# Seven block products for the latents' feed-forward up product, and the feed-forward split into two phases

## The chip, the core and the metric

One core of a Trainium2 chip runs the whole program. The metric is the device time of one execution in microseconds (us). PE is TensorE (matmuls; PEld its weight loads), DVE is VectorE, ACT is ScalarE, POOL is GpSimd, SP is the queue that issues the DMAs.

## What is computed

A two-layer backbone over 1,024 latent tokens and 256 context tokens, model width 1,024. Layer 0 mixes tokens with an mLSTM and a Hyena group, layer 1 with a gated DeltaNet and a latent-attention group. After each mixer an output projection and a gated residual give `x`; the part at issue, a convolutional feed-forward, follows:

```python
h = modulate(x, shift, scale)              # RMS norm, then scale and shift
z = dwconv(h @ w_up, conv_w, conv_b)       # 1024 -> 2 x 2816, a 3-tap convolution over tokens
y = silu(z[..., :D_FF]) * z[..., D_FF:]    # gate half and up half, D_FF = 2816
x = x + gate_mod * (y @ w_down)            # 2816 -> 1024
```

Layer 0 computes this for latents and context, layer 1 for the latents alone. All matrices are fp32. The kernel gets fp32 accuracy out of fp32r matmuls by splitting every operand into a rounded high part and a remainder: `hi*hi + hi*lo + lo*hi`, three matmuls for each pair of tiles (`mm3`, lines 229 to 231).

## The kernel before

Features lie on partitions in KT = 8 tiles of 128, tokens along the free dimension. The Tile framework puts each engine's instructions in an order of its own when the program is built: an instruction may go ahead of others that stand before it in the source, when its inputs and its buffer are free by the framework's reckoning. On the chip each engine then runs its list in that fixed order.

`emit_out` (output projection) goes over token chunks of 512, 512 and, in layer 0, 256 context tokens. While one chunk is projected, the RMS norm of the chunk before (`norm_stats`, `norm_apply`) runs in steps between the projections, and writes `h` as a high and a low tile (`hh`, `hl`). The residual `x` of all tokens (`xr`) stays in SBUF through the feed-forward.

`emit_ffn` is one loop over NF = 22 tiles `f` of the 2,816 hidden features. For each f it loads two weight tiles of 128x1024 (gate: tile f; up: tile 22+f), splits each (`load_w`: high part on ACT at line 37, low part on DVE at line 38), and makes the gate and the up product over all tokens in a PSUM tile of three banks (`big`): 8 k-tiles x 3 matmuls for each chunk. `conv3` applies the three taps with one ACT and two DVE instructions straight from PSUM, ACT applies Silu, DVE multiplies gate and up and splits the result into `yh`, `yl`. After every second f the down product of these two f is added to `xr`: for each of 8 output tiles and each chunk 6 matmuls in a PSUM bank (`sm`) and one DVE instruction (line 272). So `y` never leaves SBUF, and each down weight tile (`fdh`, `fdl`) is loaded and split once. The last f writes its up product bank by bank; then the last down blocks are made chunk by chunk, and the next norm (layer 0) or the store of the output (layer 1) is woven into them.

Buffers: raw weights, high and low parts two each (`dw`, tags `wraw`, `wh`, `wl`); PSUM two one-bank tiles (`sm`) and two three-bank tiles (`big`).

Of the kernel before, what the change touches and what calls it, by code (L numbers as in the profile page):

```python
# [8 lines left out]
F32 = mybir.dt.float32  # L9
F32R = mybir.dt.float32r  # L10
# [8 lines left out]
KT = 8  # L19
# [83 lines left out]
def norm_pads(g, h):  # L103
    for t in h:
        for c in (LAT, TP - 1):
            g.nc.gpsimd.memset(t.bitcast(F32)[:, :, c:c + 1], 0.0)


def norm_stats(g, x, chunk, pool, big, res, nm=""):
# [6 lines left out]
    for k in range(KT):  # L116
        q = sq[:, n * (1 + k % nq):n * (2 + k % nq)] if k else acc
        nc.scalar.activation(out=q, in_=x[:, k, c0:c0 + n], func=ACTF.Square)
# [24 lines left out]
def norm_apply(g, layer, which, x, h, chunk, pool, big, res, bufs=1):  # L143
# [82 lines left out]
def mm3(nc, ps, pairs):  # L226
# [7 lines left out]
def dense(g, ps, w, h, chunks, base=0):  # L234
    whi, wlo = w
    hhi, hlo = h
    for c0, n in chunks:
        mm3(g.nc, ps[:, c0 - base:c0 - base + n],
            [(whi[:, 128 * k:128 * k + 128], wlo[:, 128 * k:128 * k + 128], hhi[:, k, c0:c0 + n], hlo[:, k, c0:c0 + n])
             for k in range(KT)])  # L240


def conv3(g, ps, out, cw, cb, n):
    nc = g.nc
    stt = nc.vector.scalar_tensor_tensor
    nc.scalar.activation(out=out[:, :n], in_=ps[:, :n], func=ACTF.Identity, scale=cw[:, 1:2], bias=cb)
    stt(out=out[:, 1:n], in0=ps[:, 0:n - 1], scalar=cw[:, 0:1], in1=out[:, 1:n], op0=ALU.mult, op1=ALU.add)
    stt(out=out[:, 0:n - 1], in0=ps[:, 1:n], scalar=cw[:, 2:3], in1=out[:, 0:n - 1], op0=ALU.mult, op1=ALU.add)  # L248
# [2067 lines left out]
```

## Time and profile before

| | us |
|---|---|
| median of three runs | 3866.21 |
| lowest and highest run | 3851.93, 3870.67 |
| span of the profiled execution (first to last instruction) | 3852.7 |

Of the profiled execution only its span is given, no separate time; the span is 13.5 us below the median of the runs. The feed-forward of layer 0 with its output projection runs from about 1050 to 2120 us of the span, that of layer 1 from about 3009 us to the end. A matmul's duration in the records is longer than the distance from one start to the next, since matmuls are pipelined; the distance is what counts.

### The profile page before, as it was taken

The page shows a single profiled execution, that of the slowest core. Times are in us where ns is not written, and L with a number is a line of the kernel's source. Part 1 is how long each engine was busy: PE and PEld are TensorE (multiplying, and loading weights), DVE is VectorE, ACT ScalarE, POOL GpSimd, SP SyncE. Part 2 cuts the span into 40 slices and gives each one's busy share as a digit, 9 for nine tenths or more (in the row PEclk, how much of TensorE's full clock was granted, in tenths as well). Part 3 has the DMA queues.
Part 4 walks back from the last instruction along what each step waited for, and adds up shares of the span by engine and source line. Part 5 has one row for each costly group of instructions (what it writes and reads, how often), then busy time and mean ns, then how long its engine had stood idle before and what let it go on. Part 6 is the DMA issues. An engine that isn't in the chain of part 4 may idle for free.

```text
span 3852.7 us, 51861 instructions
## 1 busy us (share of the span) xinstructions
PE 3677.6 (95%) x20874; PEld 2982.9 (77%) x20874; DVE 2198.8 (57%) x4198; ACT 1195.1 (31%) x2221; POOL 65.3 (2%) x111
## 2 busy tenths in 40 slices
PE   6999999989999999999998999989999899999999
PEld 3778878866777888888887877767788678888887
DVE  6213566777775445444458584864566565555545
ACT  3323234511142122112224453543445332222121
POOL 0000000000000000000000000000000000000000
PEclk9999999999999999999999999996899899999999
DMA  5443556789731111011111252462355511111111
GB/s 188 129 141 123 161 178 216 215 272 307 254 121 44 39 39 39 33 33 39 44 39 66 75 153 79 143 228 101 114 178 185 181 61 50 50 44 55 39 55 60
DMA packets 303507, 440.20 MB, mean 114 GB/s; under 512 B 19546, under 2 KB 199010, under 8 KB 298276
## 3 DMA queue, kind: packets, MB, share of 16 engines
q1 hardware_dynamic: 293988, 419.07, 33.4%
q0 software_dynamic: 9280, 17.83, 1.6%
q8 instruction: 164, 2.69, 0.3%
q14 instruction: 75, 0.61, 0.0%
HBM read 334.60 MB, written 102.24 MB: 113 GB/s over the span
## 4 chain that ended last, share of the span: by engine, by line
PE 68%; DVE 5%; DMA 3%; ACT 3%; issue 2%; POOL 0%; SPq 0%; ACTq 0%; DVEq 0%; POOLq 0%
PE big L231 10%; PE big L230 10%; PE big L229 10%; PE sm L229 7%; PE sm L230 7%; PE sm L231 7%; PE maS L2005 3%; PE hyp L923 2%; PE hys L1091 1%; PE maT L1125 1%; PE hya L81 1%; DMA mw<-in_mod_w 1%; PE sd L1125 1%; PE maO L229 0%; PE pb L1620 0%
## 5 line engine op out<-in xcount | busy, mean ns | idle before, releaser
L229 PE MATMUL big<-hh,wh 128*128 128x512 f32 (+1 forms) x1728 | 639.1, 371 | 10.4 <-DVE fcg L248 9.9
L231 PE MATMUL big<-hh,wl 128*128 128x512 f32 (+1 forms) x1728 | 640.3, 371 | 0.4 <-DVE wl L38 0.4
L230 PE MATMUL big<-hl,wh 128*128 128x512 f32 (+1 forms) x1728 | 639.8, 371 | 0.1
L38 DVE TENSOR_TENSOR wl<-wraw,wh 128x1024 fp32r<-128x1024 f32 (+1 forms) x168 | 199.5, 1187 | 554.0 <-ACT wh L37 550.9
L229 PE MATMUL sm<-hh,wh 128*128 128x512 f32 (+1 forms) x1192 | 445.8, 376 | 15.7 <-ACT hh L157 5.2
L230 PE MATMUL sm<-hl,wh 128*128 128x512 f32 (+1 forms) x1192 | 441.0, 371 | 3.9 <-DVE hl L158 3.6
L231 PE MATMUL sm<-hh,wl 128*128 128x512 f32 (+1 forms) x1192 | 440.1, 370 | 0.2 <-DVE wl L38 0.2
L272 DVE SCALAR_TENSOR_TENSOR xr<-sm,modT,xr 128x512 f32<-128x512 f32 (+1 forms) x400 | 276.1, 697 | 243.4 <-PE sm L231 243.4
L229 PEld LDWEIGHTS big<-hh,wh 128*128 128x128 f32 x1728 | 325.8, 189 | 68.5 <-issue 5.5
L230 PEld LDWEIGHTS big<-hl,wh 128*128 128x128 f32 x1728 | 326.3, 189 | 59.1 <-DVE hl L158 1.3
L231 PEld LDWEIGHTS big<-hh,wl 128*128 128x128 f32 x1728 | 325.7, 189 | 56.9 <-DVE wl L38 0.7
L37 ACT ACTIVATE wh<-wraw 128x1024 fp32r<-128x1024 f32 (+1 forms) x168 | 172.7, 1028 | 598.0 <-PE big L230 441.7
L229 PE MATMUL sm<-yh,fdh 128*128 128x512 f32 (+1 forms) x800 | 298.1, 377 | 0.0
L230 PE MATMUL sm<-yl,fdh 128*128 128x512 f32 (+1 forms) x800 | 297.0, 373 | 0.0
L231 PE MATMUL sm<-yh,fdl 128*128 128x512 f32 (+1 forms) x800 | 292.5, 372 | 0.0
L229 PEld LDWEIGHTS sm<-hh,wh 128*128 128x128 f32 x1192 | 227.0, 191 | 68.5 <-issue 11.7
L230 PEld LDWEIGHTS sm<-hl,wh 128*128 128x128 f32 x1192 | 227.5, 191 | 46.0 <-DVE hl L158 7.7
L231 PEld LDWEIGHTS sm<-hh,wl 128*128 128x128 f32 x1192 | 227.1, 191 | 36.6 <-issue 0.9
L37 ACT ACTIVATE fdh<-wraw 128x1024 fp32r<-128x1024 f32 x44 | 46.6, 1059 | 555.6 <-PE sm L230 520.9
L229 PEld LDWEIGHTS sm<-yh,fdh 128*128 128x128 f32 x800 | 149.5, 188 | 44.2 <-DVE xr L272 13.8
L230 PEld LDWEIGHTS sm<-yl,fdh 128*128 128x128 f32 x800 | 150.4, 188 | 28.8 <-DVE yl L38 2.7
L231 PEld LDWEIGHTS sm<-yh,fdl 128*128 128x128 f32 x800 | 148.5, 188 | 25.9
(559 smaller groups left out, 6051.4 us busy)
## 6 DMA issues: line engine op xcount, KB each, us to landing
wraw<-in_ffn_up SPq DMA_DIRECT2D x88, 512.0 KB, 3.3
mw<-in_mod_w SPq DMA_DIRECT2D x32, 1024.0 KB, 7.7
wraw<-in_ffn_down SPq DMA_DIRECT2D x44, 512.0 KB, 3.3
dfw<-in_dft POOLq DMA_DIRECT2D x32, 512.0 KB, 7.2
wraw<-in_a_w SPq DMA_DIRECT2D x29, 512.0 KB, 3.6
wraw<-in_c_w SPq DMA_DIRECT2D x23, 512.0 KB, 3.5
win<-in_win SPq DMA_DIRECT2D x40, 256.0 KB, 3.6
mw<-in_mod_w SPq DMA_DIRECT2D x16, 512.0 KB, 4.0
```

Of the source, the lines that this page charges most:

```text
L37: nc.scalar.activation(out=hi, in_=src, func=ACTF.Copy)
L38: nc.vector.tensor_tensor(out=lo, in0=src, in1=hi.bitcast(F32), op=ALU.subtract)
L81: nc.tensor.matmul(ps[32 * c:32 * c + 32, cs], g.sc[:, k, :], wc[:, c % q], start=(k == 0), stop=(k == KT - 1), tile_position=(0, 32 * c))
L229: nc.tensor.matmul(ps, ah, bh, start=(i == 0), stop=False)
L230: nc.tensor.matmul(ps, ah, bl, start=False, stop=False)
L231: nc.tensor.matmul(ps, al, bh, start=False, stop=(i == n - 1))
L272: nc.vector.scalar_tensor_tensor(out=x[:, dt, c0:c0 + m], in0=ps[:, :m], scalar=mt[:, s, 40 + dt:41 + dt], in1=x[:, dt, c0:c0 + m], op0=AL ...
L923: nc.tensor.matmul(out, a, b, start=(i == 0), stop=(i == len(pairs) - 1))
L1091: nc.tensor.matmul(ps, wk[:, ks], mk[:, k, ms], start=(k + i == 0), stop=(k == 3 and i == 2))
L1125: g.nc.tensor.transpose(dst, src, g.ident[:src.shape[0], :src.shape[0]])
L2005: mm(S[:, ks], l, r, start=(t == 0), stop=(t == 4))
```

## The change

**Two phases.** `emit_up` makes all y of a layer and stores them, f by f, to DRAM (`g.yd`); `emit_down` then goes over the token chunks, loads the residual of the chunk (`g.xm`, stored by `emit_out`), and for each group of four f loads y for that chunk, splits it, and loads and splits the down weights again for every chunk (a tile of 4 f x 256 outputs for each pair of output tiles). Twelve matmuls (four f) go into a PSUM bank before the DVE instruction adds them to the residual.

**Seven products.** For f = 1 to 21 the latents' gate and up products together are a 2x2 block product: weights (gate, up) x two halves of the 1,024 inputs, by tokens (two halves of inputs x two chunks of 512). It is made of seven products of 4 k-tiles x 3 matmuls in place of eight. POOL makes the sums of weight halves (four adds of 128x512 for each f), which ACT and DVE then split; the three sums of token blocks (`block_sums`: `t1`, `t2`, `t4`, and the fourth, which takes the place of block (0, 1)) are made once per layer, while f = 0 runs in the plain form; DVE recombines the seven PSUM banks with seven adds of 128x512. The context tokens keep the plain form.

**Around it.** PSUM is two `sm` and six one-bank tiles (`bk`). The convolution goes bank by bank (`conv3_steps`). The norm writes `h` also in fp32 over the residual in SBUF (`keep`), since the sums need it, after the residual was stored to DRAM. In the output projection of layer 0 three weight tiles stay split in place of four, and there is one buffer less for the split inputs.

The diff, cut to its core (the host's reshape of the down weights and the renaming of `h` into blocks are left out):

```diff
+def open_sums(g, es):
+    hp = es.enter_context(g.tc.tile_pool(name="ht", bufs=1, side="right", reuse_waits="tile"))
+    return [[hp.tile([128, 4, 512], F32R, name=f"t{i}" + z) for z in "hl"] for i in (1, 2, 4)]
+def block_sums(g, h, x, sums, pool):
     nc = g.nc
+    tt = nc.vector.tensor_tensor
+    (a, b), (c, d) = [[x[j][:, 4 * i:4 * i + 4] for i in range(2)] for j in range(2)]
+    t1, t2, t4 = sums
+    tt(out=c, in0=c, in1=a, op=ALU.subtract)
+    yield 1
+    split(nc, c, *t1)
+    yield 1
+    t3 = pool.tile([128, 4, 512], F32, name="t3")
+    tt(out=t3, in0=d, in1=c, op=ALU.subtract)
+    yield 1
+    split(nc, t3, *t2)
+    yield 1
+    tt(out=b, in0=b, in1=t3, op=ALU.subtract)
+    yield 1
+    split(nc, b, *t4)
+    yield 1
+    tt(out=d, in0=t3, in1=a, op=ALU.subtract)
+    yield 1
...
+def emit_up(g, layer, h, sums, x, with_ctx, pending, close):
...
+    def product(ps, w, half, b):
+        o = 512 * half
+        mm3(nc, ps, [(w[0][:, o + 128 * k:o + 128 * k + 128], w[1][:, o + 128 * k:o + 128 * k + 128], b[0][:, k], b[1][:, k])
+                     for k in range(4)])
+    raws = load(0)
+    ws = [halves(r) for r in raws]
+    raws = load(1)
+    lat = [[bank() for _ in range(2)] for _ in range(2)]
+    dense(g, lat[0][0], ws[0], h, 0, 512)
+    drain(pending, 9 if with_ctx else 12)
+    dense(g, lat[1][0], ws[1], h, 0, 512)
+    drain(pending, 9)
+    for t in range(2):
+        dense(g, lat[t][1], ws[t], h, 512, 512)
+        drain(pending, 4)
+    t2h, t2l = sums[1]
+    ctx = [None, None]
+    drain(pending)
+    if with_ctx:
+        for t in range(2):
+            ctx[t] = small_ps(g)
+            dense(g, ctx[t], ws[t], h, LAT, CTX + 2)
+    b01 = h.blocks[0, 1]
+    split(nc, x[1][:, 4:8], *b01)
+    close()
+    with tc.tile_pool(name=f"fs{layer}", bufs=1, reuse_waits="tile") as sp, \
+            tc.tile_pool(name=f"fc{layer}", bufs=1, reuse_waits="tile") as cp:
+        T = lambda shape, tag, dt=F32, **k: sp.tile(shape, dt, tag=tag, name=tag, **k)
+        def mixes(raws, q):
+            a, b = raws
+            add = nc.gpsimd.tensor_tensor
+            s = T([128, 1024], "ws", bufs=2)
+            if q == 0:
+                add(out=s[:, 0:512], in0=b[:, 0:512], in1=b[:, 512:], op=ALU.add)
+                add(out=s[:, 512:], in0=s[:, 0:512], in1=a[:, 0:512], op=ALU.subtract)
+                mixes.s2 = s[:, 512:]
+            else:
+                add(out=s[:, 0:512], in0=a[:, 0:512], in1=b[:, 0:512], op=ALU.subtract)
+                add(out=s[:, 512:], in0=a[:, 512:], in1=mixes.s2, op=ALU.subtract)
+            t = [T([128, 1024], "ws" + z, F32R, bufs=3) for z in "hl"]
+            split(nc, s, *t)
+            return t
...
+        def up_out(f, banks, gate):
+            o = conv(banks, "u", NF + f)
+            tt(out=o[:, :n], in0=gate[:, :n], in1=o[:, :n], op=ALU.mult)
+            nc.sync.dma_start(out=g.yd[layer][f, :, 0:LAT], in_=o[:, 0:LAT])
+            if with_ctx:
+                nc.sync.dma_start(out=g.yd[layer][f, :, LAT:], in_=o[:, C0:C0 + CTX])
+        cut = 3 if with_ctx else 2
+        s12 = mixes(raws, 0)
+        w0 = halves(raws[0])
+        s34 = mixes(raws, 1)
+        gate = gate_out(0, (lat[0] + [ctx[0]])[:cut])
+        up_out(0, (lat[1] + [ctx[1]])[:cut], gate)
+        t1, t2, t4 = sums
+        for f in range(1, NF):
+            w1 = halves(raws[1], 0 if with_ctx else 512)
+            more = f + 1 < NF
+            if more:
+                raws = load(f + 1)
+            p1 = bank()
+            product(p1, w0, 0, h.blocks[0, 0])
+            s = T([128, 512], "s", bufs=2)
+            act(out=s, in_=p1, func=ACTF.Copy)
+            p6 = bank()
+            product(p6, s12, 1, t2)
+            u2 = T([128, 512], "u")
+            tt(out=u2, in0=p6, in1=s, op=ALU.add)
+            c11 = bank()
+            product(c11, w0, 1, h.blocks[1, 0])
+            if more:
+                n12 = mixes(raws, 0)
+            tt(out=c11, in0=c11, in1=s, op=ALU.add)
+            ctx = [None, None]
+            if with_ctx:
+                ctx[0] = small_ps(g)
+                dense(g, ctx[0], w0, h, LAT, CTX + 2)
+            p5 = bank()
+            product(p5, s12, 0, t1)
+            if more:
+                w0 = halves(raws[0])
+            u4 = T([128, 512], "v")
+            tt(out=u4, in0=p5, in1=u2, op=ALU.add)
+            c12 = bank()
+            product(c12, s34, 1, h.blocks[1, 1])
+            tt(out=c12, in0=c12, in1=u4, op=ALU.add)
+            gate = gate_out(f, [c11, c12, ctx[0]][:cut])
+            if with_ctx:
+                ctx[1] = small_ps(g)
+                dense(g, ctx[1], w1, h, LAT, CTX + 2)
+            p7 = bank()
+            product(p7, s34, 0, b01)
+            if more:
+                s34 = mixes(raws, 1)
+                s12 = n12
+            tt(out=u2, in0=p7, in1=u2, op=ALU.add)
+            c22 = T([128, 512], "s", bufs=2)
+            tt(out=c22, in0=p5, in1=u2, op=ALU.add)
+            c21 = bank()
+            product(c21, w1, 1, t4)
+            tt(out=c21, in0=c21, in1=u2, op=ALU.add)
+            up_out(f, [c21, c22, ctx[1]][:cut], gate)
+def emit_down(g, layer, with_ctx, after):
+    nc, tc = g.nc, g.tc
+    mt = g.modT[layer]
     ochunks = OUT_CH if with_ctx else OUT_CH[:2]
+    pending = iter(())
+    with tc.tile_pool(name=f"dx{layer}", bufs=2, reuse_waits="tile") as xp, \
+            tc.tile_pool(name=f"dy{layer}", bufs=2, reuse_waits="tile") as yp:
+        for c0, w, s in ochunks:
+            a = min(c0, LAT)
+            x = xp.tile([128, KT, 512], F32, tag="dx", name="dx")[:, :, :w]
+            nc.sync.dma_start(out=x, in_=g.xm[layer][:, :, c0:c0 + w])
+            for f0, m in DOWN_K:
+                raw = yp.tile([128, 4, 512], F32, tag="yr", name="yr")[:, :m, :w]
+                nc.sync.dma_start(out=raw, in_=g.yd[layer][f0:f0 + m, :, a:a + w].rearrange("f p n -> p f n"))
+                y = [yp.tile([128, 4, 512], F32R, tag="y" + z, name="y" + z)[:, :m, :w] for z in "hl"]
+                split(nc, raw, *y)
+                for q in range(4):
+                    wr = g.wp.tile([128, 1024], F32, tag="wraw", name="wraw")[:, :256 * m]
+                    nc.sync.dma_start(out=wr.rearrange("p (f c) -> p f c", c=256), in_=g.ap["ffn_down"][layer, q, :, f0:f0 + m])
+                    wt = [g.wp.tile([128, 1024], F32R, tag="w" + z, name="w" + z)[:, :256 * m] for z in "hl"]
+                    split(nc, wr, *wt)
+                    for dt in (2 * q, 2 * q + 1):
+                        ps = g.bank.tile([128, 512], F32, tag="bk", name="bk")[:, :w]
+                        o = 128 * (dt % 2)
+                        mm3(nc, ps, [(wt[0][:, 256 * i + o:256 * i + o + 128], wt[1][:, 256 * i + o:256 * i + o + 128],
+                                      y[0][:, i], y[1][:, i]) for i in range(m)])
+                        nc.vector.scalar_tensor_tensor(out=x[:, dt], in0=ps, scalar=mt[:, s, 40 + dt:41 + dt], in1=x[:, dt],
+                                                       op0=ALU.mult, op1=ALU.add)
+                        drain(pending, 1)
+            drain(pending)
+            pending = after((c0, w, s), x)
+        drain(pending)
...
-def emit_out(g, layer, x, xsrc, wname, ks, ochunks, np_, after):
+def emit_out(g, layer, xp, xsrc, wname, ks, ochunks, np_, after):
-    with tc.tile_pool(name="oum", bufs=len(ks) + 2, reuse_waits="tile") as mp:
+    with tc.tile_pool(name="oum", bufs=len(ks) + 1, reuse_waits="tile") as mp:
...
             drain(pending)
+            nc.sync.dma_start(out=g.xm[layer][:, :, c0:c0 + w], in_=x)
...
+def emit_ffn(g, layer, xsrc, wname, ks, with_ctx, down):
...
+    xs, pending = emit_out(g, layer, xp, xsrc, wname, ks, OUT_CH if with_ctx else OUT_CH[:2], np_,
+                           lambda ch, x, big: norm_chunk(g, layer, 1, lambda k: x[:, k], h, ch, np_, big, keep=ch[2] == 0))
+    sums = open_sums(g, ss)
+    emit_up(g, layer, h, sums, xs, with_ctx, chain(pending, block_sums(g, h, xs, sums, np_)), xs_.close)
+    ss.close()
+    bs.close()
+    emit_down(g, layer, with_ctx, down(ws))
+    return ws, pss
```

## Rows read from the trace of the kernel before

**Rows 1.** Page, part 1: busy us (share of span) and count by engine.
```profile
PE 3677.6 (95%) x20874; PEld 2982.9 (77%) x20874; DVE 2198.8 (57%) x4198; ACT 1195.1 (31%) x2221; POOL 65.3 (2%) x111
```
**Rows 2.** Windows: us, busy us and count by engine, PE clock, DMA share, GB/s.
```profile
1200.00:2000.00 800.00, 800.00 (x4082) 670.52 (x4080) 392.57 (x405) 153.39 (x130) 0.00 (x0) 1.00 0.11 37
3200.00:3800.00 600.00, 600.00 (x2623) 490.43 (x2622) 307.69 (x308) 136.13 (x128) 0.00 (x0) 1.00 0.15 48
```
**Rows 3.** Timeline of DVE, layer 0: start us, us, instruction, [idle before].
```profile
1518.32 1.23 DVE L38 TENSOR_TENSOR wl<-wraw,wh 128x1024 fp32r<-128x1024 f32 x1 [5.20 <-ACT wh L37]
1519.63 1.55 DVE L247 SCALAR_TENSOR_TENSOR fcg<-big,fcw,fcg 128x1281 f32<-128x1281 f32 x1
...
1532.34 1.23 DVE L38 TENSOR_TENSOR wl<-wraw,wh 128x1024 fp32r<-128x1024 f32 x1 [9.57 <-ACT wh L37]
```
**Rows 4.** Timeline of DVE, layer 1.
```profile
3416.35 1.23 DVE L38 TENSOR_TENSOR wl<-wraw,wh 128x1024 fp32r<-128x1024 f32 x1 [3.53 <-ACT wh L37]
...
3427.23 1.23 DVE L38 TENSOR_TENSOR wl<-wraw,wh 128x1024 fp32r<-128x1024 f32 x1 [7.14 <-ACT wh L37]
```
**Rows 5.** Timeline of PE, the context part of a product of layer 0.
```profile
1259.97 0.28 PE L229 MATMUL big<-hh,wh 128*128 128x258 f32 x1
1260.09 0.28 PE L230 MATMUL big<-hl,wh 128*128 128x258 f32 x1
```
**Rows 6.** Groups of DVE by form: busy us, mean ns, idle before with releasers.
```profile
L38 DVE TENSOR_TENSOR wl<-wraw,wh 128x1024 fp32r<-128x1024 f32 x156 | 191.3, 1226 | 549.9 <-ACT wh L37 546.8 <-PE sm L1125 1.9
L272 DVE SCALAR_TENSOR_TENSOR xr<-sm,modT,xr 128x256 f32<-128x256 f32 x80 | 38.8, 485 | 43.7 <-PE sm L231 43.7
L296 DVE TENSOR_TENSOR fcu<-fcg,fcu 128x1024 f32<-128x1024 f32 x21 | 25.7, 1225 | 0.7
L158 DVE SCALAR_TENSOR_TENSOR hl<-nbig,modT,hh 128x512 fp32r<-128x512 f32 x32 | 23.0, 747 | 1.0
L955 DVE TENSOR_TENSOR t<-hyp,hcp 128x512 f32<-128x512 f32 x32 | 20.3, 682 | 11.3 <-PE hyp L923 11.2
L964 DVE TENSOR_TENSOR t<-U,kin 128x2048 f32<-128x2048 f32 x8 | 18.3, 2293 | 3.4 <-DMA kin<-klat 3.3
...
L516 DVE SCALAR_TENSOR_TENSOR oco<-sm,hcws,oco 128x511 f32<-128x511 f32 x16 | 11.7, 745 | 4.7 <-ACT oed L515 4.7
...
L2013 DVE RECIPROCAL sm<-sm 128x1 f32<-128x1 f32 x32 | 5.0, 157 | 5.0 <-ACT P L2012 4.2
```
**Rows 7.** Groups of POOL.
```profile
L1649 POOL TENSOR_TENSOR sm<-sm,oi 128x512 f32<-128x512 f32 x8 | 10.2, 1278 | 126.5 <-DVE oi L1645 115.5 <-issue 11.0
```
**Rows 8.** Groups of ACT by form.
```profile
L37 ACT ACTIVATE wh<-wraw 128x1024 fp32r<-128x1024 f32 x156 | 165.2, 1059 | 588.7 <-PE big L230 438.1 <-PE sm L230 145.9 <-issue 2.1
```
**Rows 9.** Timelines of DVE: end of the norms, layer 0 and layer 1.
```profile
1152.91 0.88 DVE L158 SCALAR_TENSOR_TENSOR hl<-nbig,modT,hh 128x256 fp32r<-128x256 f32 x2 [0.19 <-ACT hh L157]
...
3130.16 1.42 DVE L158 SCALAR_TENSOR_TENSOR hl<-nbig,modT,hh 128x512 fp32r<-128x512 f32 x2
```
**Rows 10.** Windows around the end of f = 0, and the end of layer 0.
```profile
1155.00:1165.00 10.00, 4.99 (x22) 4.13 (x22) 9.16 (x7) 7.90 (x7) 0.00 (x0) 0.74 0.15 52
...
2040.00:2120.00 80.00, 68.89 (x312) 53.33 (x311) 69.54 (x165) 34.07 (x59) 0.79 (x4) 0.95 0.22 77
3800.00:3830.00 30.00, 27.44 (x114) 21.72 (x113) 15.98 (x19) 8.34 (x10) 0.00 (x0) 0.94 0.02 6
```
**Rows 11.** Timeline of PE, end of f = 0 in layer 1.
```profile
3138.49 0.77 PE L229 MATMUL big<-hh,wh 128*128 128x512 f32 x1 [4.92 <-DVE fcg L248]
...
3142.47 0.63 PE L229 MATMUL big<-hh,wh 128*128 128x512 f32 x1
```
**Rows 12.** Page, part 6: DMA issues, KB each, median us from issue to landing.
```profile
mw<-in_mod_w SPq DMA_DIRECT2D x32, 1024.0 KB, 7.7
wraw<-in_ffn_down SPq DMA_DIRECT2D x44, 512.0 KB, 3.3
```

More of the change, by code (lines that the diff above doesn't have):

```diff
@@ L140, in norm_spread, with norm_apply @@
     return bc
-def norm_apply(g, layer, which, x, h, chunk, pool, big, res, bufs=1):
+def norm_apply(g, layer, which, x, h, chunk, pool, big, res, bufs=1, keep=False):
     nc = g.nc
@@ L223, in load_w, with mm3 @@
     return hi, lo
-def mm3(nc, ps, pairs):
+def mm3(nc, ps, pairs, first=True):
     n = len(pairs)
@@ L231, in mm3, with dense @@
         nc.tensor.matmul(ps, al, bh, start=False, stop=(i == n - 1))
-def dense(g, ps, w, h, chunks, base=0):
+def dense(g, ps, w, h, c0, n):
     whi, wlo = w
[L236 to L243, printed above, removed]
-    nc = g.nc
[L245 to L248, printed above, removed]
@@ L251, with open_blocks @@
-OUT_CH = [(0, 512, 0), (512, 512, 0), (C0, CTX, 1)]
-def emit_ffn(g, layer, x, h, with_ctx, after, pending):
+    mm3(g.nc, ps[:, :n], [(whi[:, 128 * k:128 * k + 128], wlo[:, 128 * k:128 * k + 128], *h.pair(k, c0, n)) for k in range(KT)])
+OUT_CH = [(0, 512, 0), (512, 512, 0), (C0, CTX, 1)]
+DOWN_K = [(f, min(4, NF - f)) for f in range(0, NF, 4)]
+def open_blocks(g, es, with_ctx):
+    hp = es.enter_context(g.tc.tile_pool(name="hb", bufs=1, side="right", reuse_waits="tile"))
+    tiles = lambda nm, n, k=4: [hp.tile([128, k, n], F32R, name=nm + z) for z in "hl"]
+    ctx = tiles("bx", CTX + 2, KT) if with_ctx else None
+    return Blocks({(i, j): tiles(f"b{i}{j}", 512) for i in range(2) for j in range(2)}, ctx)
@@ new lines, in emit_up, with load, halves @@
+    tt = nc.vector.tensor_tensor
+    act = nc.scalar.activation
+    up_w = lambda j: g.ap["ffn_up"][layer, j]
+    bank = lambda: g.bank.tile([128, 512], F32, tag="bk", name="bk")
+    cw = lambda j: (g.fcw[:, layer, j, :], g.fcb[:, layer, j:j + 1])
+    def load(f):
+        raws = []
+        for j in (f, NF + f):
+            raw = g.wp.tile([128, 1024], F32, tag="wraw", name="wraw")
+            nc.sync.dma_start(out=raw, in_=up_w(j))
+            raws.append(raw)
+        return raws
+    def halves(raw, lo=0):
+        t = [g.wp.tile([128, 1024], F32R, tag="w" + z, name="w" + z) for z in "hl"]
+        split(nc, raw[:, lo:], t[0][:, lo:], t[1][:, lo:])
+        return t
@@ L2149, in store, with last, after @@
+    ds, pss = emit_ffn(g, 0, g.xp, "a_wo", range(4, 8), True, next_layer)
+    ns.close()
+    emit_odd(g, h2[0], ds, pss)
+    def last(ws):
+        def after(ch, x):
+            c0, w, s = ch
             for k in range(KT):
-                nc.sync.dma_start(out=out[:, k, c0:c0 + n], in_=x[:, k, c0:c0 + n])
+                nc.sync.dma_start(out=out[:, k, c0:c0 + w], in_=x[:, k])
             return iter(())
-        emit_ffn(g, 1, x, h, False, store, pending)
+        return after
+    ds, pss = emit_ffn(g, 1, g.xd, "c_wo", range(8), False, last)
```

213 lines of the change are left out of this document (80 added, 133 removed).

## The prediction

> **What bounds the kernel now.** The page's first part comes first: PE is busy 95% of the span, DVE 57%, ACT 31%, POOL 2% [rows 1]. An average over stages decides nothing, so the windows of the two feed-forward loops are next: PE is busy in all of both, at the full granted clock, 2.4 GHz, while DVE is busy 49 and 51%, ACT 19 and 23%, DMA 11 and 15% [rows 2]. So each matmul taken out of these loops is worth its spacing, as long as nothing else becomes late. The spacing is read from what waits for a product of known size. In layer 0, `wl` reuses a weight buffer that one product over all tokens frees: 14.02 us apart for 48 matmuls of 512 columns and 24 of 258 [rows 3]. The 258-column ones start 0.12 us apart [rows 5], which leaves (14.02 - 24 x 0.12)/48 = 0.232 us for one of 512. In layer 1 it is 10.88/48 = 0.227 us [rows 4]. These groups also show that the order on an engine is not the source's: the source splits a weight before the product that uses it, yet the split at 1518.32 stands ahead of a convolution of the f before [rows 3]. The program builder moves work forward when its buffer is free, and I count on that below.
>
> **What is saved.** For f = 1 to 21 seven products of 12 matmuls replace eight: 12 less per f, 252 per layer. 252 x 0.232 = 58.4 and 252 x 0.227 = 57.2: **-115.5**. All down matmuls, the context ones and f = 0 stay.
>
> **Does DVE keep pace in the new loop?** A period of PE becomes 84 x 0.227 = 19.1 us in layer 1 and 84 x 0.232 + 48 x 0.12 = 25.3 in layer 0. DVE in layer 1, from [rows 6]: three full splits, 3 x 1.226 = 3.7, and a half one, 0.69 (half of 1.226, rounded up by a fixed part; the 512-wide L955 took 0.682); seven adds that read PSUM at 0.682, 4.8 (three also write PSUM, which no row shows; between 0.682 and the 0.745 of L516 it changes the sum by 0.2); eight taps at 0.745, 6.0; four one-column ones at 0.157, 0.6; the product 1.225. That is 17.0 us, 17.9 with 0.04 between dependent ones. In layer 0 half a split, four context taps at 0.485 and the longer product come on top: 19.8, about 20.9 with gaps. So DVE fills 94% in layer 1, 83% in layer 0, against about half now. Its work comes in lumps, but six banks let it lag by two products. ACT (four splits at 1.06 [rows 8], and copies and taps of about half that size) stays under 12 us. POOL: four adds at 1.278 [rows 7] = 5.1 us. The longest chain through them (split of `w1` after the last product of the f before, about 6 us; load 3.3 [rows 12]; two adds 2.6; split 2.3) is ready some 15 us after the start of an f, and its result is needed at 19.1 + 2.7. So I see no wait in the steady loop, but little room: I take 10 us for layer 1 and 3 for layer 0: **+13**, bounds 0 and (next) what a blocked DVE costs.
>
> On GpSimd beside VectorE no row decides: the eight POOL adds ran 1.278 us each [rows 7], with little beside them. The Trainium skill (SBUF — State Buffer, section "Who interferes with whom") says that a VectorE instruction with two SBUF inputs and a GpSimd instruction that reads SBUF exclude each other, and that whoever comes second waits for the whole of the other. By that rule the splits, the product and the taps of the one block kept in SBUF could each wait behind a POOL add; the first rival prices it.
>
> **Seam 1, from f = 0 to f = 1.** The product with `t2` needs every norm, the sums and their splits. DVE makes them after the norm: seven instructions of 128x2048 at 2.293 [rows 6] = 16.0 us. Then two POOL adds 2.6 (their buffers lie where the residual was, so they wait for its last reader), an ACT split 1.06 and a DVE split 1.23: 20.9 us after the norm. In layer 1 the norm ends at 3130.16 + 1.42 = 3131.6 [rows 9], so this is ready at 3152.5. PE is through f = 0 at 3138.49 - 4.92 = 3133.6 [rows 11]; two products that need neither (w0 with blocks (0,0) and (1,0)) cover 5.4. Idle 13.5, in place of 4.9 now, and some 2.5 for banks that wait on the convolution of f = 0, which stands behind the sums: +11. In layer 0 the norm ends at 1153.8 [rows 9], ready at 1174.7; PE ends f = 0 near 1157 and covers 5.5; idle 12.5 in place of 5.0 (10 us less 4.99 busy [rows 10]): +9 with the banks. **+20** together; bounds 0 (if PE finds other work) and +45 (sums late, `keep` waiting for the store of the residual).
>
> **Seam 2, from up to down.** Nothing of the kind exists now. When PE ends the last product, DVE and ACT still do its add, taps and product, about 6 us. The first y buffers lie where those tiles were. So: loading 1 MB of y, 7.7 us as for a 1 MB weight [rows 12], can start when the block sums' tiles are free, some 4 us in; then ACT splits 2048 columns (2 x 1.06 = 2.1) and DVE 2.3. 4 + 7.7 + 4.4 = 16; I take 15. Bounds: 4.4 if only the split is exposed, 22 if store, load and split run in a row. After an idle time of this kind the clock comes back late: behind the 4.92 us the next nine matmuls took 3.98 us [rows 11] in place of 2.0, which is the 1.2 GHz level. +2 each. What the last f costs now (2.6 of 30 us in layer 1 [rows 10], taken alike in layer 0) goes. 2 x 17 - 2 x 2.6 = **+29**, bounds +8 and +45.
>
> **Down phase.** Same matmuls. For latents a pair of output tiles takes 24 x 0.23 = 5.5 us of PE against one weight split and two adds on DVE, under 3.5. In the context chunk of layer 0 it takes 24 x 0.12 = 2.9 us. One load and its split occupy a raw buffer for 3.3 + 1.06 + 1.23 and waits, about 7; with two buffers that is 3.5 per pair. DVE also makes the norm of latent chunk 1 there, 16 x 0.747 + 7 x 0.68 and small ones, 18 us. 24 pairs x 0.5 = **+12**, bounds 0 and +25.
>
> **Rest.** At the end of layer 0 the norms of the latents are woven into the last 22 us of down work now, and PE is idle 80 - 68.89 = 11.1 us [rows 10]; afterwards only the context norm is uncovered, and the next projection's latent products stand ready. Less the 2.6 already counted, and leaving 2.5: **-6**. The output projection splits a weight tile twice more and has one input buffer less: **+2**, bounds 0 and +5.
>
> Sum: -115.5 + 13 + 20 + 29 + 12 - 6 + 2 = **-45.5**. The profiled span, 3852.7, becomes 3807; it lies 13.5 under the median of the runs, so the median becomes 3866.2 - 45.5 = **3821 us**. About 0.5% (19 us, also the spread of the three runs) can be told from no change.
>
> **Rivals.**
> 1. *DVE becomes the bound.* Each POOL add stops DVE for its whole time: 17.9 + 5.1 = 23.0 us per f in layer 1, above 19.1 and above the 96 x 0.227 = 21.8 of now; 26.0 against 25.3 in layer 0. (23.0 - 19.1) x 21 + 0.7 x 21 = 97 in place of the 13: 3821 + 84 = **3905**, slower. It decides from a period of 21.7 in layer 1 on (45.5/21 = 2.2 above 19.5). For it: 94%. Against: only about 7 us of DVE's work has two SBUF inputs, and nothing makes all four adds meet it.
> 2. *Nothing is exposed.* The builder fills the seams, DVE keeps up: -115.5 + 8 + 5 + 5 - 6 = -104 at best, say **3770**. For it: PE was never idle in the loops [rows 2]. Against: at the seams little else is ready.
> 3. *The seams cost double*, 49 more: **3870**, no change. For it: the residual's 2 MB and y share the queue. Against: the loads of one seam are 3 MB at most.
> 4. *The builder leaves the source's order in the down phase*: the splits of y and of the next weights stand behind the adds that wait for PE, 1.2 us for three pairs and 3.6 for y in each of 30 groups: 30 x 7.2 = 216, **about 4025**. Against: [rows 3].
>
> **Chances.** Forecast 0.54 (own range 3785 to 3855; of it 0.05 within 0.5%), rival 1 0.13, rival 2 0.14, rival 3 0.14 (0.09 the same, 0.05 slower), rival 4 0.05. Faster 0.49 + 0.14 = 0.63; same 0.05 + 0.09 = 0.14; slower 0.13 + 0.05 + 0.05 = 0.23. The range, **3765 to 3895**, takes in rivals 2 and 3 and the milder half of rival 1.
>
> **What the profile after will show.** Windows of the loops: PE at 100%, f to f 19.1 us in layer 1 and 25.3 in layer 0, if right; PE under 95% with waits on DVE or on PSUM banks under rival 1, with DVE instructions longer than in [rows 6] where POOL runs. PE's matmul count falls by 504. The timeline should have one gap of some 10 us behind f = 0 and one of some 15 us before the first down matmul in each layer, with half-clock matmuls behind them. The context chunk of layer 0 should run at the pace of its weight splits. The prediction fails most easily at DVE's 94%, then at the length of seam 2.

## The result and the profile after

The changed kernel takes 3875.52 us in the median of its runs, beside 3853.66 us for the kernel before: a ratio of 1.0059, 95% interval [1.0037, 1.0080]. It is slower by 0.6%, some 22 us, where 45 us faster was forecast. The profiled execution has a span of 3888.2 us, 35.5 above that of before; its own time, 3890.0, lies 14.5 above the median.

Page, part 1, of the kernel after, then windows of its loop in layer 0, its loop in layer 1, and the seams between up and down of both layers (columns as in [rows 2]):

```profile
PE 3601.2 (93%) x20370; PEld 2912.9 (75%) x20370; DVE 2504.6 (64%) x4880; ACT 1444.1 (37%) x2664; POOL 284.2 (7%) x279
```

```profile
1200.00:1700.00 500.00, 500.00 (x2604) 425.22 (x2603) 371.43 (x560) 202.63 (x280) 102.61 (x80) 1.00 0.20 69
3200.00:3590.00 390.00, 365.74 (x1548) 292.48 (x1548) 283.73 (x439) 151.18 (x223) 91.63 (x72) 0.99 0.21 73
...
1715.00:1745.00 30.00, 9.51 (x31) 6.77 (x30) 12.47 (x14) 7.03 (x7) 0.00 (x0) 0.61 0.72 256
3596.00:3630.00 34.00, 9.05 (x30) 6.51 (x29) 14.52 (x19) 8.14 (x8) 0.00 (x0) 0.60 0.68 243
```

The 504 matmuls are gone (20874 in [rows 1]). In layer 0 the loop is as forecast: PE always busy. In layer 1 PE, never idle before [rows 2], is busy 365.74 of 390 us, while DVE is busy only 73%: no engine is full. At the seams PE stands still for most of 30 us and its mean granted clock is 0.6, a mixture of 2.4 and 1.2 GHz.

PE's waits after, by stretch (us in total, times, longest): first seam of layer 0, of layer 1; loop of layer 1; second seams; down phase of layer 1 and of layer 0:

```profile
PE sm L166 <- DVE ndg L165: 15.5, 2, 15.1
...
PE bk L253 <- ACT wsh L64: 13.5, 1, 13.5
...
PE bk L253 <- DVE fcg L662: 23.2, 14, 2.9
...
PE bk L253 <- ACT yh L64: 20.2, 1, 20.2
...
PE bk L253 <- ACT yh L64: 24.7, 1, 24.7
PE bk L253 <- ACT wh L64: 8.0, 1, 8.0
...
PE bk L253 <- ACT wh L64: 9.6, 7, 2.9
PE bk L255 <- DVE wl L65: 5.9, 7, 2.7
```

For layer 1's loop the forecast saw no wait and only set 10 us aside. Timelines of PE (the start of an f), DVE, POOL and ACT show one turn:

```profile
3406.50 0.39 PE L253 MATMUL bk<-b00h,wh 128*128 128x512 f32 x1
...
3418.33 0.69 DVE L65 TENSOR_TENSOR wl<-wraw,wh 128x512 fp32r<-128x512 f32 x1
...
3422.67 1.29 POOL L363 TENSOR_TENSOR ws<-wraw 128x512 f32<-128x512 f32 x1 [16.39 <-DMA wraw<-in_ffn_up]
3423.91 1.30 POOL L367 TENSOR_TENSOR ws<-wraw 128x512 f32<-128x512 f32 x1
3425.16 1.28 POOL L364 TENSOR_TENSOR ws<-ws,wraw 128x512 f32<-128x512 f32 x1
...
3426.48 1.06 ACT L64 ACTIVATE wsh<-ws 128x1024 fp32r<-128x1024 f32 x1 [4.25 <-POOL ws L364]
...
3427.57 1.33 DVE L65 TENSOR_TENSOR wsl<-ws,wsh 128x1024 fp32r<-128x1024 f32 x1 [5.09 <-ACT wsh L64]
...
3439.86 0.69 DVE L65 TENSOR_TENSOR wl<-wraw,wh 128x512 fp32r<-128x512 f32 x1
```

The split of `w1` (3418.33) frees the raw buffers; the next load lands; POOL makes three adds, the third of which (L364) completes what the first split needs; ACT splits; DVE, which has stood idle 5.09 us for that, splits at 3427.57. Behind this split in DVE's order stand the block adds, the gate convolution (whose bank PE waits for), the up convolution, and at their end the next split of `w1`. 9.24 us to the split of the sums and 12.29 from there: a closed loop of 21.53 us, where PE has work for 19.3. From the second f on, 18 of the 19 distances between these splits of `w1` are 21.3 to 21.6 us.

### The profile page after: what moved, and what is told of

The parts are those of the page before. It is cut to its first block, busy times and chain, and to the rows that moved or that the text cites. A ratio compares the mean times of both kernels' runs of the same rounds, so it can differ in the third digit from the quotient of the medians.

```text
span 3888.2 us, 53052 instructions
## 1 busy us (share of the span) xinstructions
PE 3601.2 (93%) x20370; PEld 2912.9 (75%) x20370; DVE 2504.6 (64%) x4880; ACT 1444.1 (37%) x2664; POOL 284.2 (7%) x279
## 4 chain that ended last, share of the span: by engine, by line
PE 53%; DVE 12%; DMA 6%; ACT 4%; issue 4%; POOL 2%; SPq 0%; POOLq 0%; ACTq 0%; DVEq 0%
PE bk L255 9%; PE bk L254 9%; PE bk L253 9%; PE sm L253 3%; PE sm L254 3%; PE sm L255 3%; PE maS L2152 3%; DMA wraw<-in_ffn_up 1%; DVE wl L65 1%; PE hyp L1067 1%; PE maT L1269 1%; DMA wraw<-in_ffn_down 1%; PE hys L1235 1%; DVE wsl L65 1%; POOL ws L363 1%
## 5 line engine op out<-in xcount | busy, mean ns | idle before, releaser
L253 PE MATMUL bk<-yh,wh 128*128 128x512 f32 (+1 forms) x880 | 334.8, 382 | 62.6 <-ACT yh L64 44.9
L253 PE MATMUL sm<-hh,wh 128*128 128x512 f32 x832 | 339.1, 408 | 8.5 <-ACT hh L184 4.1
L254 PE MATMUL sm<-hl,wh 128*128 128x512 f32 x832 | 334.9, 403 | 2.6 <-DVE hl L185 2.5
L255 PE MATMUL bk<-yh,wl 128*128 128x512 f32 (+1 forms) x880 | 329.3, 379 | 6.0 <-DVE wl L65 5.9
L255 PE MATMUL sm<-hh,wl 128*128 128x512 f32 x832 | 333.9, 402 | 0.3 <-DVE wl L65 0.3
L254 PE MATMUL bk<-yl,wh 128*128 128x512 f32 (+1 forms) x880 | 332.9, 379 | 0.5 <-DVE yl L65 0.5
L474 DVE SCALAR_TENSOR_TENSOR dx<-bk,modT,dx 128x512 f32<-128x512 f32 (+1 forms) x240 | 166.0, 696 | 193.7 <-PE bk L255 192.8
L253 PEld LDWEIGHTS bk<-yh,wh 128*128 128x128 f32 x880 | 170.3, 194 | 98.8 <-ACT yh L64 45.8
L255 PEld LDWEIGHTS bk<-yh,wl 128*128 128x128 f32 x880 | 168.2, 192 | 41.5 <-DVE wl L65 9.2
L254 PEld LDWEIGHTS bk<-yl,wh 128*128 128x128 f32 x880 | 169.6, 193 | 34.2 <-DVE yl L65 1.9
```

Of the source, the lines that this page charges most:

```text
L253: nc.tensor.matmul(ps, ah, bh, start=(i == 0), stop=False)
L254: nc.tensor.matmul(ps, ah, bl, start=False, stop=False)
L255: nc.tensor.matmul(ps, al, bh, start=False, stop=(i == n - 1))
L474: nc.vector.scalar_tensor_tensor(out=x[:, dt], in0=ps, scalar=mt[:, s, 40 + dt:41 + dt], in1=x[:, dt], op0=ALU.mult, op1=ALU.add)
```

## The experiments

Ratios are to the kernel before, timed beside each run.

**Four raw buffers in layer 1's loop.**
```diff
-raw = g.wp.tile([128, 1024], F32, tag="wraw", name="wraw")
+raw = g.wp.tile([128, 1024], F32, tag="wrv" if f > 1 and f % 2 == 0 and not with_ctx else "wraw", name="wraw")
```


> Edit: in layer 1 the two raw weight tiles of every second f get buffers of their own, so a load no longer waits until VectorE has split w1 of the f before; the arithmetic is the same, nothing else is changed. Theory A (a loop of latencies: split of w1, load, POOL adds, split of the sums, and VectorE's own queue behind them sets 21.4 us per f): the period of an f falls to 19.1 to 19.6 us, the PE waits of 1.8 to 1.9 us in it go, and the kernel is 35 to 44 us faster than the changed kernel, near 3835. Theory B (VectorE's throughput, or its stops beside POOL's adds, sets the period): the period stays at 21 us or more and the time within 8 us of 3875.

3847.99 us, 0.9963 [0.9945, 0.9982]: about 37 us below the changed kernel (1.0059 - 0.9963 = 0.0096 of 3859; by PE's timelines layer 1 shrinks by 36, from 491.8 to 455.7 us between the first matmul of f = 0 and the end of up). PE has no wait left in the loop, shown by its window:
```profile
3200.00:3550.00 350.00, 350.00 (x1519) 284.97 (x1518) 285.69 (x433) 151.28 (x217) 94.08 (x66) 1.00 0.22 79
```
A period is 84 x 350/1519 = 19.35 us (19.37 between two splits of `w1`), and DVE is 82% full. Theory A holds: a loop of latencies, not throughput.

**The context norm ahead of the sums, layer 0.**
```diff
-tt(out=c, in0=c, in1=a, op=ALU.subtract)
+one = pool.tile([128, 1], F32, name="one")   # from the context norm's r: 0*r + 1
+nc.vector.tensor_scalar(one, res[-1][:, 0:1], 0.0, 1.0, op0=ALU.mult, op1=ALU.add)
+nc.vector.scalar_tensor_tensor(out=c, in0=c, scalar=one, in1=a, op0=ALU.mult, op1=ALU.subtract)
```


> Edit: the first block difference of layer 0 takes a factor of one that is made from the context norm's result, so the sums come behind the small steps of that norm; the output is the same. Theory A (the order put the long sums between the steps, each step waited for one): the PE stall of 15.1 us at the first seam of layer 0 falls to under 5 us, the half clock behind it goes, and the kernel is 10 to 17 us faster than the changed kernel. Rival (the sums are simply 18 us of VectorE work that must be done somewhere before the second product): the stall moves to the first product that reads a sum and the time stays within 4 us.

3875.01 us, 1.0033 [1.0014, 1.0051]: some 10 us below the changed kernel, at theory A's lower end, but the two intervals overlap. The trace is clearer: f = 0 of layer 0 takes 39.1 us for 51.0. In the changed kernel DVE went on in this way from 1150 us, one small step of the context norm and one long block sum or split in turn:
```profile
1155.34 0.15 DVE L79 TENSOR_TENSOR nw2t<-nw2t,nw2n 128x2 f32<-128x2 f32 x1
1155.41 2.28 DVE L65 TENSOR_TENSOR t1l<-xr,t1h 128x2048 fp32r<-128x2048 f32 x1
```
The 15.1 us wait is gone; what is left in that stretch:
```profile
PE sm L254 <- DVE bxl L185: 4.4, 3, 1.9
PE bk L255 <- DVE wl L65: 2.5, 1, 2.5
```

**Two phases alone.** Every up product is plain, as before; sums, POOL adds and the split of `b01` are left out.
```diff
-p1 = bank()
-product(p1, w0, 0, h.blocks[0, 0])
...
+for c in range(2):
+    ps.append(bank())
+    dense(g, ps[c], ws[t], h, 512 * c, 512)
```

> Edit: the two phases stay, with y in DRAM, but both layers compute the up product as before, with all 24 matmuls per block row and no sums, no POOL adds, no seven products. Theory A (the two phases alone cost what stands at the seam between up and down and in the down phase: 20 and 25 us of idle, some 27 us in the down stages, about 10 us at the first chunk): 50 to 65 us slower than the kernel before, 3905 to 3920. Rival (two phases are nearly free, and the loss of the change lies in the seven products): within 15 us of the kernel before.

3859.46 us, 1.0002 [0.9985, 1.0018]. My theory fell: the two phases alone cost nothing that can be measured. The stall between up and down is not there at all, by the windows of the same seams (the 2.9 us in the second one are a later wait of the down phase, for a bank that the add to the residual frees) and by SyncE's timeline:
```profile
1715.00:1745.00 30.00, 30.00 (x156) 25.70 (x155) 13.39 (x20) 8.16 (x12) 0.22 (x4) 1.00 0.24 79
...
3590.00:3620.00 30.00, 27.08 (x111) 21.61 (x110) 13.25 (x17) 6.73 (x8) 0.00 (x0) 0.94 0.62 226
```
```profile
1581.41 0.37 SPq L482 DMA_DIRECT2D yr<-yd  x1
```
The first y group is loaded 157 us before the first down matmul (1738.8), into memory that the plain form leaves unused. In the changed kernel SyncE issues it behind the last stores of y:
```profile
1725.08 0.33 SPq L387 DMA_DIRECT2D yd<-fcu  x1
...
1725.93 0.79 SPq L458 DMA_DIRECT2D dx<-xm  x1
1728.43 1.11 SPq L461 DMA_DIRECT2D yr<-yd  x2
```
With the plain form as a base, PE's timelines split the change by stage (first matmul of f = 0, of f = 1, last of up, first and last of down). Layer 0: f = 0 grows from 29.5 to 51.0 us, the 21 others shrink from 582.4 to 531.4 (25.31 us each; before 2 x 14.02 [rows 3]), the seam takes 20.2, down stays (349.8 and 348.8): 10 us gained. Layer 1: f = 0 from 28.8 to 34.1, the others 458.1 and 457.7 (the 13.5 us wait is in them), that is, all 57 us saved are lost, the seam takes 24.7, down 260.8 and 259.5: 28 us lost.

**Seven products in layer 0 only**: the same edit under `if not with_ctx`, that is, in layer 1.

> Edit: the seven products in layer 0 alone; layer 1 computes its up product plainly in the two phases. Theory A (in layer 1 the seven products take away 57 us of matmuls and bring 48 us of waits in the loop and some 9 us at its first seam): 0 to 8 us faster than the changed kernel, 3867 to 3875. Rival (layer 1's seven products gain there, and the loss of the kernel is elsewhere): 20 us or more slower than the changed kernel.

3853.85 us, 0.9978 [0.9959, 0.9997]: 31 us below the changed kernel, more than either theory gave. The sign is theory A's; its sum lacked layer 1's seam, which goes too.

**Other places for the down pools.**
```diff
-with tc.tile_pool(name=f"dx{layer}", bufs=2) as xp, tc.tile_pool(name=f"dy{layer}", bufs=2) as yp:
+with tc.tile_pool(name=f"dy{layer}", bufs=2) as yp, tc.tile_pool(name=f"dx{layer}", bufs=2, side="right") as xp:
```


> Edit, against the changed kernel: in the down phase the pool of the y groups is opened first and the pool of the residual on the other side of SBUF, so that the first y group lies where the sums of weights lay and not where the last gate and up rows lie; no transfer and no arithmetic is changed. Theory A (the first load of y waits for memory that the last f of the up phase still uses): the PE stalls of 20.2 and 24.7 us between up and down fall to under 8 us each, and the kernel is 25 to 38 us faster than the changed kernel, 3837 to 3850. Rival (the round trip through DRAM, store of the last row, then load, sets the stall): the stalls stay above 15 us and the time within 8 us of the changed kernel.

3873.48 us, 1.0040 [1.0020, 1.0060]; stalls 22.4 and 19.7 us. A miss for theory A; the time is the rival's. But SyncE's waits and timeline at the first seam show neither the memory nor the round trip of the last row as what holds the first load:
```profile
SPq L387 <- DVE fcu L386: 16.7, 1, 16.7
```
```profile
1721.94 19.57 SPq L461 DMA_DIRECT2D yr<-yd  x4
```
SyncE stands 16.7 us before the last store of y, until DVE has made that row; the first load of y, which reads f = 0 to 3 and needs none of that row, comes behind it in the queue and goes out 8.5 us after PE's last product (1713.4). It lands some 12 us later.

**The same, with y loaded by GpSimd.** Besides, y, its high and its low part lie one behind the other, and layer 0's next norm pool on the other side.
```diff
-nc.sync.dma_start(out=raw, in_=g.yd[layer][f0:f0 + m, ...])
+nc.gpsimd.dma_start(out=raw, in_=g.yd[layer][f0:f0 + m, ...])
```


> Edit, against the changed kernel: the y groups of the down phase lie where the sums of weights lay (in that order: y, its high part, its low part), and their loads are issued by GpSimd and not by SyncE; no other edit. In the other placement alone the loads of y still stood behind the last store of y in SyncE's order, and the stalls of 20 and 25 us stayed. Theory A (the load stands behind that store in the queue of one engine): the stalls fall to under 8 us each and the kernel is 22 to 35 us faster than the changed kernel, 3847 to 3860. Rival (the first y load takes its 9 to 14 us beside the residual and weight loads wherever it is issued): the stalls stay above 12 us.

3844.92 us, 0.9970 [0.9957, 0.9983]: 34 us below the changed kernel. The waits for `yh` at the two seams, and GpSimd's timeline of layer 0:
```profile
PE bk L253 <- ACT yh L64: 3.6, 1, 3.6
...
PE bk L253 <- ACT yh L64: 5.3, 1, 5.3
```
```profile
1709.52 0.80 POOL L462 DMA_DIRECT2D yr<-yd  x1 [0.31 <-issue]
```
The first load goes out 8 us before up ends (1717.4) and no longer behind the last store, which SyncE issues at 1723.26. So the stall was a place in a queue. This run also changed the order of the y buffers, so the two runs alone do not part queue and place; SyncE's wait in the run before does.

**First sums of weights early, layer 1**: `s1`, `s2` of odd f get a pool that is open before the residual's; on top of the four raw buffers.
```diff
-s12 = mixes(raws, 0)
+s12 = mixes(raws, 0) if with_ctx else first   # first: made ahead of f = 0's products, in the new pool
```


> Edit, on top of the raw weight buffers of the first experiment: in layer 1 the sums of weights s1 and s2 of every odd f get tiles of their own, which are free before the block sums are done, so the first ones are made during f=0. Theory A (the first POOL adds of layer 1 wait only for the memory of the normalised x): the PE stall of 13.5 us before the first product of sums falls to under 6 us, and the kernel is 7 to 13 us faster than the first experiment's, near 3838. Rival (the stall is the block sums themselves, t2 not being split before then): the stall stays above 9 us and the time within 4 us of the first experiment's.

3843.42 us, 0.9967 [0.9952, 0.9983], as without it (0.9963): the time is the rival's. The 13.5 us wait is gone, but others took its place, and f = 0 grew from 31.5 to 36.1 us:
```profile
PE bk L253 <- ACT s L415: 6.8, 1, 6.8
...
PE bk L254 <- DVE t2l L65: 1.6, 1, 1.6
```
ACT's copy of `p1` writes tile `s`, which lies in the same memory of the residual, free only after the last block sum. Moving one of the tiles moved the wait to the next.

**Four raw buffers for the down weights.**
```diff
-wr = g.wp.tile([128, 1024], F32, tag="wraw", name="wraw")[:, :256 * m]
+wr = (yp.tile([128, 1024], F32, tag="wr2", name="wr2") if q % 2 else g.wp.tile([128, 1024], F32, tag="wraw", name="wraw"))[:, :256 * m]
```


> Edit, against the changed kernel: in the down phase the raw tiles of the down weights come from four buffers and not two; nothing else. Theory A (in the context chunk of layer 0 and at the chunk switch of layer 1 a weight load waits for its buffer, or stands behind stores, and PE waits for it): the 15.5 us of idle in the context chunk fall to under 5 us, and the kernel is 10 to 20 us faster than the changed kernel, 3855 to 3865. Rival (the split on ScalarE and VectorE or the DMA rate sets it): within 5 us of the changed kernel.

3843.84 us, 0.9969 [0.9955, 0.9984]: 35 us, twice what was expected. Of the 15.5 us of idle that were to fall to under 5, 8.9 stay: one wait of 7.0 us for the low part of a weight, which DVE makes, is the most of it. Down shrinks from 348.8 to 331.1 us in layer 0 and from 259.5 to 250.1 in layer 1, and layer 1's seam by 4.4. In the changed kernel the 8.0 us wait at layer 1's chunk switch is a load of weights behind seven stores of output in SyncE's queue, by SyncE's and ACT's timelines:
```profile
3744.64 7.09 SPq L2309 DMA_DIRECT2D out_dram<-dx  x7
3751.83 0.94 SPq L466 DMA_DIRECT2D wraw<-in_ffn_down  x2
...
3757.51 1.06 ACT L64 ACTIVATE wh<-wraw 128x1024 fp32r<-128x1024 f32 x1 [4.97 <-DMA wraw<-in_ffn_down]
```

**Order of POOL's adds.**
```diff
-add(out=s[:, 0:512], in0=a[:, 0:512], in1=b[:, 0:512], op=ALU.subtract)
+add(out=s[:, 0:512], in0=b[:, 512:], in1=mixes.s2, op=ALU.subtract)
```


> Edit, against the changed kernel: in both layers the first half of the second pair of weight sums is formed from the sum s2 and not from the raw weights (equal but for rounding), so that POOL finishes the sums for the next f's first product before it starts that pair; raw weight buffers as in the changed kernel. Theory A (a loop of latencies through one POOL add more than it needs): the split of those sums starts 1.3 us earlier, and the period of 21.4 us in layer 1 falls by 0.8 to 1.5 us, 16 to 30 us in all. Rival (another link sets the loop: VectorE's order behind it, or the load): the period stays within 0.4 us.

3882.77 us, 1.0068 [1.0051, 1.0085]: nothing gained, and the period stays, as the rival had it. The first split did come earlier, but DVE then waits for the second one (timelines of POOL and DVE):
```profile
3418.98 1.30 POOL L367 TENSOR_TENSOR ws<-wraw,ws 128x512 f32<-128x512 f32 x1
3420.23 2.28 POOL L368 TENSOR_TENSOR ws<-wraw,ws 128x512 f32<-128x512 f32 x1
...
3420.03 1.33 DVE L65 TENSOR_TENSOR wsl<-ws,wsh 128x1024 fp32r<-128x1024 f32 x1 [3.79 <-ACT wsh L64]
...
3423.64 1.23 DVE L65 TENSOR_TENSOR wsl<-ws,wsh 128x1024 fp32r<-128x1024 f32 x1 [1.02 <-ACT wsh L64]
```
From the split of `w1` (3412.08) to the next (3433.44) it is 21.36 us. The builder keeps both splits early in DVE's order, so all four adds lie in the loop, the last one at 2.28 us.

**The adds on DVE**, with four raw buffers.
```diff
-add = nc.gpsimd.tensor_tensor
+add = nc.vector.tensor_tensor if not with_ctx else nc.gpsimd.tensor_tensor
```


> Edit, on top of the raw weight buffers of the first experiment: in layer 1 the four sums of weights of each f are made by VectorE (four of 0.70 us) and not by GpSimd (four of 1.3 us). Theory A (VectorE is not the bound: 82% busy at 19.3 us per f, 96% with the sums): the period stays at 19.3 to 19.8 us and the time within 12 us of the first experiment's 3848. Rival (GpSimd's adds hold VectorE up for their whole time, as beside the small operations of the norm): with them gone from GpSimd the loop is no slower though VectorE does more, and its other operations get shorter by more than 1 us per f. Other rival (in-order VectorE is so full that each wait is passed on): period above 20.3 us, 20 us or more slower than the first experiment's.

3844.87 us, 0.9970 [0.9957, 0.9983], as with POOL. PE stays full with DVE at 326.85/350 = 93%:
```profile
3200.00:3550.00 350.00, 350.00 (x1519) 284.95 (x1518) 326.85 (x506) 152.38 (x217) 0.00 (x0) 1.00 0.22 80
```
Without its 72 adds (about 0.685 us each) DVE is busy about 277 us here, for 285.69 beside POOL's adds: POOL costs DVE some 0.5 us per f, less than the 1 us of the first rival. So neither DVE's load nor POOL beside it was the bound.

**Combinations.** The first: four raw buffers in both places, context norm first, early sums, other places.

> All edits together: four raw weight buffers in layer 1's loop, the sums of layer 0 behind the context norm, early tiles for the first sums of weights in layer 1, the other placement of the down pools, four raw buffers in the down phase. If the losses are separate places in time, as the theories say, the savings add: 37 us for the loop, 10 for the first seam of layer 0, 10 for that of layer 1, 32 for the second seams, 12 for the down phase, 3775 to 3790, or 0.978 to 0.983 of the kernel before. Rival (what one wait gives back the next takes, the matmul clock or VectorE above all): above 3815.

3796.59 us, 0.9844 [0.9819, 0.9870]: some 6 us short of theory A, but far from the rival. Seams of 19.3 and 13.3 us stay, as the placement alone had shown. The second loads y by GpSimd:

> All edits of the combination before, with this placement and the y loads issued by GpSimd. Theory A: the stalls of 19.3 and 13.3 us between up and down that were left fall to under 8 us each, 3770 to 3782, or 0.976 to 0.980 of the kernel before. Rival (as in the run beside it): no more than 5 us below the combination before, 3792 to 3800.

3803.64 us, 0.9867 [0.9848, 0.9886]: the rival's side. In layer 0 the wait for `yh` is 3.6 us, and a new one for weights took its place (waits of PE, then SyncE's timeline):
```profile
PE bk L253 <- ACT wh L64: 18.3, 2, 17.7
```
```profile
1711.61 1.10 SPq L403 DMA_DIRECT2D yd<-fcu  x1
1712.75 0.69 SPq L472 DMA_DIRECT2D dx<-xm  x1
1713.48 16.83 SPq L482 DMA_DIRECT2D wr<-in_ffn_down  x3
```
The second weight tile stood behind the last stores and 2 MB of residual, and ACT could split it only at 1727.64. In layer 1 the wait is named `yh`, 17.5 us, but has the same cause: the split of y stands behind that of the second weight tile in ACT's order. The third gives the first two tiles the buffers that are free before (`q > 1` for `q % 2`):

> The second combination, with one change: of the four weight tiles of a y group the first two come from the weight buffers that are free before the up phase ends, and the last two from the new ones (before, every second one). Theory A (in the second combination the weights of the second product, in memory freed last, stood behind the last store in SyncE's order, and the stall only moved from y to them): the stalls of 17.7 us in layer 0 and 17.5 us in layer 1 fall to under 6 us each, and the kernel is 18 to 28 us faster than the first combination, 3768 to 3780, or 0.976 to 0.980. Rival (the burst of transfers at the seam takes its time whatever stands first): within 6 us of the first combination, 3790 to 3803.

3790.92 us, 0.9819 [0.9802, 0.9836]: the lowest median, 67 us below before (3858.14), though its interval overlaps that of the first combination. Both seams are 3.6 us, so what stood ahead of these loads in the queue was the cause of the stalls; but of 25 us gained there against the first combination (19.3 + 13.3 - 7.2), 15 came back in the down phases (340.5 for 329.5 us, 254.3 for 250.1): waits for y's low part (2.3 and 2.6 us) and for later weights (4.8 us the longest that is new), with a granted clock of 0.81 and 0.88 in the 40 us behind the seams for 0.95 and 0.92. The stalls went as theory A had it, the time is the rival's.

**Two phases alone, four down buffers** (the new ones for `q > 1`).

> Edit, on top of the plain two phases of the third experiment: the four raw buffers of the down weights. Theory A (what two buffers cost in the down phase is the same with the plain up phase): 28 to 36 us faster than the plain two phases, 3823 to 3831, or 0.991 to 0.993 of the kernel before; the two phases by themselves then gain. Rival (that gain came from the seam, which the plain form does not have): within 10 us of the plain two phases.

3839.99 us, 0.9943 [0.9920, 0.9965]: some 23 us below the plain form (1.0002), 5 short of theory A; down shrinks by 17.6 and 9.4 us, as with seven products. The two buffers' loss belongs to the two phases.

## Why the prediction was wrong

- **Saving, -115.5: nearly right.** 504 matmuls less; 25.31 us per f in layer 0 for 25.3; 19.35 in layer 1, when nothing waits, for 19.1, which is some 5 us less saved.
- **Loop, +13: the step that failed most.** "So I see no wait in the steady loop" set the chain through the POOL adds against PE's need alone. The chain was to be ready some 15 us after the start of an f; it took 22.4 (3406.50 to 3428.90), because the split of `w1` ended 12.5 us into the f for 6 and because three adds, not two, stood before the split of the sums. Even so its result was there before PE could use it (3430.6); what PE waited for was the bank that the gate convolution frees behind that split in DVE's order. The chain's end is a split in the middle of DVE's in-order queue; the next link of the chain, the split of `w1`, stands 12.29 us behind it in that queue, so chain and queue close a loop of 21.5 us. It cost 37 us in layer 1, not 10 (four raw buffers, shown), and nothing in layer 0, not 3. DVE's work itself was well sized: 285.69/350 x 19.35 = 15.8 us for 17.0; and at 93% it is no bound.
- **Seam 1, +20: cause half right.** Layer 1's idle time is 13.53 us for 13.5, in part by luck: from the end of the norm it is 14.3 us to the last block sum for 16.0, then three POOL adds take 6.1 (one of them 3.31, beside the split of `b01`) for two of 2.6 together, PE covers one product and not two, and f = 0 itself is 5.3 us longer than in the plain form, which no term held. POOL's first add does wait for the last block sum (until 3152.36), as the prediction had it; but freeing that one tile only moved the wait, and no run took the block sums themselves away from this place. Layer 0: f = 0 grew by 21.6 us over the plain form, for 9 forecast. The sum assumed that the context norm ends first; the order put a sum or split of 2.28 us between its small steps. Putting it first gave about 10 us back.
- **Seam 2, +29: size off.** 20.2 and 24.7 us for 15 each. The mechanism as written (memory free some 4 us in) was the lesser part: the loads of y stood behind the last store in SyncE's queue, so that store, load and split ran in a row though the load does not need that store. The prediction had priced that at 22 and kept it as a bound. Shown by the placement alone, which changed little while SyncE stood before that store, and with the load on GpSimd.
- **Down phase, +12: half.** Its mechanism (two raw buffers) was right for most of the waits in layer 0's context chunk, 7.0 us of which stay with four; 27 us in both layers went with four buffers, layer 1's chunk switch among them, which no term held.
- **End of layer 0 and output projection, -4: small**, not tested apart.

The misses are about 24 (loop), 12 (seam 1, layer 0), 15 (seam 2) and 15 (down): 66 us, beside the 67 between -45 and +22. They were sized from the places above, not independently, and the 5 us each of the saving and of layer 1's f = 0 are not among them, so the close match is partly luck. Rival 1 fell with four raw buffers, where POOL's adds still ran and PE was full, and with the adds on DVE. In absolute time rival 3 (3870) came nearest, by a part of its mechanism; but it was meant as no change, and +22 us lies about midway between it (+4) and rival 1 (+39). The seven products are worth 48 us, give or take some 11 (0.9943 - 0.9819 = 0.0124 of 3858), where most waits are taken away, for 115.5 of matmul time.

## What to carry to other kernels

A chain through several engines is judged by where its last link stands in each in-order queue, not by when its result is needed: follow it once round until it comes back to its first instruction, and compare that with the period. At a phase change, list for each queue what stands ahead of the next phase's first load (a store that waits for the last result, 2 MB that nobody needs yet), and lay the first tiles of the new phase, all of them, into memory that is free before. And test the scaffolding without the idea: the plain two phases showed in one run which losses belonged to which.

## What the runs showed of the hardware

Small DVE operations took seven times as long beside POOL's adds. Timelines of POOL and DVE, first seam of layer 0 after:
```profile
1166.87 3.32 POOL L363 TENSOR_TENSOR ws<-wraw 128x512 f32<-128x512 f32 x1 [105.14 <-DVE nw2t L77]
1170.15 1.25 POOL L367 TENSOR_TENSOR ws<-wraw 128x512 f32<-128x512 f32 x1
...
1166.78 2.28 DVE L65 TENSOR_TENSOR b01l<-xr,b01h 128x2048 fp32r<-128x2048 f32 x1
1168.98 1.22 DVE L79 TENSOR_TENSOR nw2t<-nw2t,nw2n 128x2 f32<-128x2 f32 x1
1170.24 1.19 DVE L81 SCALAR_TENSOR_TENSOR nr<-nw2t,nr 128x2 f32<-128x2 f32 x1
...
1172.68 0.16 DVE L79 TENSOR_TENSOR nw2t<-nw2t,nw2n 128x2 f32<-128x2 f32 x1
```
POOL's add, begun 0.09 us into a DVE split, takes 3.32 us, about the split's remaining 2.19 and its own 1.25; then each 128x2 operation of 0.16 us ends only when the running add does (1170.19, 1171.40) and takes 1.2. This is the rule that the prediction cited from the Trainium skill (SBUF — State Buffer, section "Who interferes with whom"), and the trace agrees with it. In the steady loop it costs little: the same 350 us of full PE with the adds on either engine.

The prediction held that no row of before decides this. One does, by the timelines of POOL and DVE:
```profile
2994.17 1.27 POOL L1649 TENSOR_TENSOR sm<-sm,oi 128x512 f32<-128x512 f32 x1 [0.64 <-DVE oi L1645]
```
```profile
2994.95 2.90 DVE L38 TENSOR_TENSOR wl<-wraw,wh 128x1024 fp32r<-128x1024 f32 x2 [0.85 <-ACT wh L37]
```
Two splits that begin 0.49 us before the end of a POOL add take 2.90 us in place of 2 x 1.23.
